# Attention over strided keys: row sums ahead of use, scaling on three engines, and stores of 64 rows of 16 KiB between single loads

## The chip, the cores and the metric

The kernel runs on one core of a Trainium2 chip. The metric is the device time of one execution in microseconds (us). Executions of a program on one core carry the state "fast" when they lie within 1.5% of the fastest of the same kernel, and "slow" above; comparisons below use fast ones.

## The reference

Q, K and V are float32 arrays of 8 x 12 x 1024 x 64. Only every 64th row of K and V takes part, so each of the 96 heads has 16 keys and 16 values, and all 1024 queries of a head attend to the same 16.

```python
def reference(Q, K, V, stride):              # stride = 64
    batch, heads, seq, dim = Q.shape
    scale = 1.0 / np.sqrt(dim)
    for i in range(seq):
        attend_positions = np.arange(0, seq, stride)
        ...
        scores = np.einsum('bhqd,bhkd->bhqk', q, k) * scale
        weights = np.exp(scores - np.max(scores, axis=-1, keepdims=True))
        weights = weights / (np.sum(weights, axis=-1, keepdims=True) + 1e-10)
        result[:, :, i, :] = np.einsum('bhqk,bhkd->bhqd', weights, v)[:, :, 0, :]
```

So 25 MB of Q must be read and 25 MB of output written, with little arithmetic on each byte.

## The kernel before

It works in 24 groups of four heads. A group is one load of 1 MiB of Q, a cast on POOL, a transpose on VectorE, scores on PE, exponentials on ScalarE, sums and outputs on PE, the division on VectorE, and one store of 1 MiB. All transfers are issued by one queue, in order. These parts matter here:

```python
    QBUFS = 10        # groups of Q that can be loaded or on their way
    OBUFS = 9         # buffers of results
    ...
    def sums(g):                                   # 8 matmuls of 4 columns
        sm = psum_s.tile([P, 2, 8, 2], FP32, name="sm", tag="sm")
        for i in range(8):
            nc.tensor.matmul(sm[:, :, i], lhsT=wt[g][:, i], rhs=s_sel, ...)
        nc.vector.reciprocal(rec[g], sm.rearrange("p b i e -> p b (i e)"))

    def outputs(g, c):                             # c = 0 to 3, 512 columns each
        ...
        nc.vector.tensor_tensor(out=out_sb[g][:, :, 4 * c : 4 * c + 4],
                                in0=ps..., in1=rec[g]..., op=ALU.mult)

    def store(g):                                  # 128 rows (partitions) of 8 KiB
        o = out_sb[g]
        _copy(nc, _ap_with(out, [[16 * D, P], [2 * SD, 2], [1, 16 * D]], g * HG * SD),
                  _ap_with(o, [o.ap[0], [1, 1], [1, 32 * D]]))
    ...
    for g in range(NG):
        ...
        store(g)
        if g + QBUFS < NG:
            load(g + QBUFS)
```

"Row" of a store means one partition of the on-chip memory; a store of 128 rows touches all 128 partitions.

The softmax here doesn't subtract the row's maximum and nothing guards it: scores larger than these inputs give would overflow.

## Time and profile before

| | before |
|---|---|
| median of 3 runs | 129.8 us (129.72 to 129.88) |
| span of the profiled run | 127.7 us |
| VectorE / POOL busy | 109.2 us (85%) / 66.7 us (52%) |
| moved over the span | 51.23 MB, 401 GB/s |

The issuing queue's timeline (start, length, issuer, transfer) shows how early stores were queued; loads lie between these lines.

```profile
23.59 0.63 SPq L35 DMA_DIRECT2D out_dram<-out_sb  x1
...
27.57 0.59 SPq L35 DMA_DIRECT2D out_dram<-out_sb  x1
...
31.56 0.59 SPq L35 DMA_DIRECT2D out_dram<-out_sb  x1
```

The ten first loads run until 31.1 us, and the first packet of the first store starts at 30.45 us, so that store was queued 6.2 us ahead of its turn.

### The profile page before, as it was taken

The numbers are of one execution on the slowest core, as the hardware profiler recorded it, in microseconds if no ns is written. First come the engines' busy times: TensorE is split into PE (matmuls) and PEld (weight loads), VectorE is DVE, ScalarE is ACT, GpSimd is POOL, SyncE is SP. The second block draws the span as 40 slices with busy tenths as digits, with TensorE's granted clock in tenths as the row PEclk, the third lists the DMA queues.
The fourth block names the chain that finished last, engine by engine and source line by source line (L and its number), as shares of the span: only waits on it lengthen the run. The fifth ranks groups of instructions, "written<-read, shape, count | busy, mean of one in ns | idle before, by whom it ended". The sixth has DMA issues, their size and how long they took to land. (4 is left out here: it accounts for less than half of the span.)

```text
span 127.7 us, 1518 instructions
## 1 busy us (share of the span) xinstructions
PE 73.3 (57%) x508; PEld 38.6 (30%) x508; DVE 109.2 (85%) x170; ACT 39.6 (31%) x55; POOL 66.7 (52%) x69
## 2 busy tenths in 40 slices
PE   0006767974476097866675579755567776674000
PEld 0003233441433063333342234432234323342000
DVE  6997468999979987899999999999999999999500
ACT  3003404224244134344424440444431344323000
POOL 8980499675217605387767635787555727000000
PEclk9999999999779855599999965799998559999555
DMA  2999989898998998989989999999999999999981
GB/s 70 380 322 459 482 339 482 349 482 359 462 472 336 503 400 377 505 346 431 493 344 439 454 385 436 441 408 452 426 398 464 385 421 431 426 416 428 421 372 46
DMA packets 7913, 51.23 MB, mean 401 GB/s; under 512 B 3872, under 2 KB 3872, under 8 KB 3872
## 3 DMA queue, kind: packets, MB, share of 16 engines
q1 hardware_dynamic: 7904, 51.12, 96.8%
q8 instruction: 4, 0.07, 0.2%
q14 instruction: 5, 0.04, 0.1%
HBM read 25.95 MB, written 25.17 MB: 400 GB/s over the span
## 5 line engine op out<-in xcount | busy, mean ns | idle before, releaser
L254 DVE TENSOR_TENSOR out_sb<-o_ps,rec 128x512 f32<-128x512 f32 x96 | 59.9, 685 | 4.8 <-PE o_ps L249 2.6
L229 ACT ACTIVATE w<-sc 64x512 bf16<-64x512 f32 x48 | 35.1, 732 | 60.0 <-PE sc L218 56.7
L207 POOL CAST qb<-qn 128x2048 bf16<-128x2048 f32 x24 | 45.5, 1898 | 0.4 <-DMA qn<-in_Q_dram 0.4
L249 PE MATMUL o_ps<-vb,w 128*128 128x256 bf16 x192 | 38.0, 321 | 2.4 <-DVE out_sb L254 1.4
L199 POOL TENSOR_TENSOR vb<-mask,v_rep 128x256 bf16<-128x256 bf16 x24 | 16.1, 670 | 40.3 <-PE o_ps L249 35.4
L218 PE MATMUL sc<-qt,k_t 128*128 128x512 bf16 x96 | 32.7, 472 | 1.5 <-DVE qt L211 1.2
L211 DVE STREAM_TRANSPOSE qt<-qb 128x1024 int32<-128x1024 int32 x24 | 29.7, 1237 | 1.6 <-POOL qb L207 1.6
L249 PEld LDWEIGHTS <-w 128*128 128x128 bf16 x192 | 19.3, 110 | 16.2 <-issue 8.6
L238 PE MATMUL sm<-s_sel,w 128*128 128x4 bf16 x192 | 8.7, 167 | 22.1 <-ACT w L229 22.1
L238 PEld LDWEIGHTS <-w 128*128 128x128 bf16 x192 | 6.9, 100 | 30.1 <-ACT w L229 29.6
L218 PEld LDWEIGHTS <-k_t 128*128 128x128 bf16 x96 | 10.8, 114 | 12.0 <-issue 6.5
L169 PE MATMUL kp<-perm_k,k_m 128*128 128x128 bf16 x24 | 3.1, 311 | 17.5 <-DVE k_m L161 17.5
L242 DVE RECIPROCAL rec<-sm 128x32 f32<-128x32 f32 x24 | 7.8, 326 | 0.3 <-PE sm L238 0.3
L169 PEld LDWEIGHTS <-k_m 128*128 128x128 bf16 x24 | 2.3, 141 | 18.2 <-DVE k_m L161 18.2
L177 ACT CAST k_t<-kp 128x512 bf16<-128x512 f32 x6 | 3.2, 590 | 14.1 <-PE kp L169 14.1
L161 DVE TENSOR_SCALAR k_m<-k_raw,slot_m 128x256 bf16<-128x256 f32 x12 | 6.8, 626 | 0.0
L192 DVE CAST v_rep<-vp 128x384 bf16<-128x384 f32 x4 | 2.2, 558 | 2.6 <-PE vp L188 2.6
L135 POOL MEMSET k_t<- 128x4608 bf16 x1 | 3.9, 3938 | 0.0
L145 DVE TENSOR_SCALAR s_sel<-col,slot_f 128x4 bf16<-128x4 int16 x1 | 3.2, 3155 | 0.1
L188 PE MATMUL vp<-v_bf,perm_v 128*128 128x384 bf16 x4 | 2.0, 489 | 0.8 <-DVE v_rep L192 0.6
L177 ACT ACT_TABLE_LOAD x1 | 1.3, 1283 | 2.1 <-DVE k_t L129 2.1
L129 DVE MEMSET k_t<- 128x1152 uint32 x1 | 1.0, 1018 | 1.0 <-PEq L314 1.0
(17 smaller groups left out, 6.3 us busy)
## 6 DMA issues: line engine op xcount, KB each, us to landing
qn<-in_Q_dram SPq DMA_DIRECT2D x24, 1024.0 KB, 13.9
out_dram<-out_sb SPq DMA_DIRECT2D x24, 1024.0 KB, 12.0
k_raw<-in_K_dram SPq DMA_DIRECT2D x1, 384.0 KB, 4.1
v_raw<-in_V_dram SPq DMA_DIRECT2D x1, 384.0 KB, 7.2
```

Source lines behind the costliest of these rows:

```text
L161: nc.vector.tensor_scalar(out=k_m[:, 4 * m : 4 * m + 4, :, h], in0=kr, scalar1=slot_m[:, h : h + 1], scalar2=None, op0=ALU.mult,)
L169: nc.tensor.matmul(kp[:, i, :, f], lhsT=k_m[:, 4 * m + 2 * u + i, f].rearrange("p h q -> p (h q)"), rhs=perm_k.rearrange("p c a b k -> p c ...
L177: nc.scalar.copy(_ap_with(dst, [dst.ap[0], [KW, 8], [32, 4], [1, NK]], extra_offset=NK), kp.rearrange("p i c f (s k) -> p (i c f) s k", s=4),)
L199: nc.gpsimd.tensor_tensor(out=vb[g], in0=mask, in1=v_rep[:, g // 2, g % 2].unsqueeze(1).to_broadcast([P, 4, D]), op=ALU.mult,)
L207: nc.gpsimd.tensor_copy(out=qb[g], in_=qn[g])
L211: nc.vector.transpose(qt[g].bitcast(I32), qb[g].bitcast(I32))
L218: nc.tensor.matmul(sc, lhsT=k_t[:, g, f, NK * (1 - e) : NK * (1 - e) + P], rhs=_ap_with(q, [q.ap[0], [2 * D, 8], [16 * D, 2], [2, 32]], ex ...
L229: nc.scalar.activation(out=_ap_with(wa, [wa.ap[0], [P, 8], [1, 2], [2, 32]], extra_offset=64 * a), in_=sc[64 * a : 64 * a + 64].rearrange( ...
L238: nc.tensor.matmul(sm[:, :, i], lhsT=wt[g][:, i], rhs=s_sel, start=True, stop=True)
L242: nc.vector.reciprocal(rec[g], sm.rearrange("p b i e -> p b (i e)"))
L249: nc.tensor.matmul(ps[:, :, i], lhsT=wt[g][:, 2 * c + i], rhs=vb[g].rearrange("p s d -> p (s d)"), start=True, stop=True,)
L254: nc.vector.tensor_tensor(out=out_sb[g][:, :, 4 * c : 4 * c + 4], in0=ps.rearrange("p b i (e d) -> p b (i e) d", e=2), in1=rec[g][:, :, 4 ...
```

## The change

The change intends to take work off VectorE and to halve the number of packets in a store. Sums are made one group ahead, by four matmuls of 256 columns and a transpose. Of each group's scaling, VectorE keeps three quarters; the last quarter is copied out by ScalarE and multiplied on POOL. Key and value preparation is cut into small steps. Two groups share one result buffer of 2 MiB, and each pair leaves in two stores of 1 MiB: partitions 0 to 63 first, then 64 to 127, each row 16 KiB long, with one load after each. The core of the diff, with cuts:

```diff
-    OBUFS = 9
+    OBUFS = 4
...
-            nc.tensor.matmul(
-                sm[:, :, i], lhsT=wt[g][:, i], rhs=s_sel, start=True, stop=True
-            )
+                sm[32 * q : 32 * q + 32], lhsT=sel32,
+                rhs=wt[g][:, :, 32 * q : 32 * q + 32],
...
+        nc.vector.transpose(
+            smt.rearrange("p i r -> p (i r)"), sm.rearrange("p i r -> p (i r)")
+        )
...
+        if n < 4:
+            nc.scalar.copy(part(i0 + n, 4 - n), ps[:, n:4])
+            nc.gpsimd.tensor_tensor(
+                out=part(i0 + n, 4 - n), in0=part(i0 + n, 4 - n),
+                in1=fact(i0 + n, 4 - n), op=ALU.mult,
+            )
...
-    def store(g):
-        o = out_sb[g]
-            _ap_with(out, [[16 * D, P], [2 * SD, 2], [1, 16 * D]], g * HG * SD),
-            _ap_with(o, [o.ap[0], [1, 1], [1, 32 * D]]),
+    def store(n, h):
+        o = out_2[n][64 * h : 64 * h + 64]
+            _ap_with(out, [[16 * D, 64], [2 * SD, 4], [1, 16 * D]],
+                2 * n * HG * SD + h * SD),
+            _ap_with(o, [o.ap[0], [1, 1], [1, 64 * D]]),
...
-        store(g)
-        if g + QBUFS < NG:
-            load(g + QBUFS)
+        if g % 2 == 1:
+            for h in range(2):
+                store(g // 2, h)
+                if g - 1 + h + QBUFS < NG:
+                    load(g - 1 + h + QBUFS)
```

More of the change, by code (lines that the diff above doesn't have):

```diff
@@ L82 @@
     psum_sc = ctx.enter_context(tc.tile_pool(name="psc", bufs=2, space=bass.MemoryType.PSUM))
-    psum_o = ctx.enter_context(tc.tile_pool(name="po", bufs=4, space=bass.MemoryType.PSUM))
+    psum_o = ctx.enter_context(tc.tile_pool(name="po", bufs=2, space=bass.MemoryType.PSUM))
     psum_s = ctx.enter_context(tc.tile_pool(name="psm", bufs=2, space=bass.MemoryType.PSUM))
@@ L147 @@
     )
+    sel32 = const.tile([P, 32], BF16, name="sel32")
+    nc.vector.memset(sel32, 0.0)
+    nc.vector.tensor_copy(out=sel32[:, 0:4], in_=s_sel)
     slot_m = const.tile([P, 4], FP32, name="slot_m")
@@ L155, with key_rows @@
     v_rep = const.tile([P, NC, 2, D], BF16, name="v_rep")
-    def keys(m):
+    def key_rows(m):
         kr = k_raw[:, 4 * m : 4 * m + 4].rearrange("p n (q f) -> p n f q", f=2)
@@ L164, in keys @@
             )
-        for u in range(2):
-            kp = psum_o.tile([P, 2, 2, 2, 4 * NK], FP32, name="kp", tag="o")
-            for i in range(2):
-                for f in range(2):
-                    nc.tensor.matmul(
-                        kp[:, i, :, f],
-                        lhsT=k_m[:, 4 * m + 2 * u + i, f].rearrange("p h q -> p (h q)"),
-                        rhs=perm_k.rearrange("p c a b k -> p c (a b k)"),
-                        start=True, stop=True,
-                    )
-            g0 = 8 * m + 4 * u
-            dst = k_t[:, g0 : g0 + 4]
-            nc.scalar.copy(
-                _ap_with(dst, [dst.ap[0], [KW, 8], [32, 4], [1, NK]], extra_offset=NK),
-                kp.rearrange("p i c f (s k) -> p (i c f) s k", s=4),
-            )
@@ L183, in value_rows @@
-    def value_rows():
-        nc.vector.tensor_copy(out=v_bf, in_=v_raw)
-        for n in range(2):
-            for c in range(2):
-                vp = psum_sc.tile([P, NC // 2, D], FP32, name="vp", tag="sc")
-                nc.tensor.matmul(
-                    vp, lhsT=perm_v[:, c].rearrange("p a b e k -> p (a b e k)"),
-                    rhs=v_bf[:, 6 * n : 6 * n + 6], start=True, stop=True,
-                )
-                nc.vector.tensor_copy(out=v_rep[:, 6 * n : 6 * n + 6, c], in_=vp)
@@ L194, with keys @@
-    qb, qt, wt, vb, rec, out_sb = {}, {}, {}, {}, {}, {}
+    def keys(m):
+        kp = psum_o.tile([P, 4, 2, 2, 4 * NK], FP32, name="kp", tag="o")
+        for i in range(4):
+            for f in range(2):
+                nc.tensor.matmul(
+                    kp[:, i, :, f],
+                    lhsT=k_m[:, 4 * m + i, f].rearrange("p h q -> p (h q)"),
+                    rhs=perm_k.rearrange("p c a b k -> p c (a b k)"),
+                    start=True, stop=True,
+                )
+        dst = k_t[:, 8 * m : 8 * m + 8]
+        nc.scalar.copy(
+            _ap_with(dst, [dst.ap[0], [KW, 16], [32, 4], [1, NK]], extra_offset=NK),
+            kp.rearrange("p i c f (s k) -> p (i c f) s k", s=4),
+        )
@@ L197, in values, with value_rows @@
+    def value_rows(n):
+        for c in range(2):
+            vp = psum_s.tile([P, NC // 2, D], FP32, name="vp", tag="sm")
+            nc.tensor.matmul(
+                vp, lhsT=perm_v[:, c].rearrange("p a b e k -> p (a b e k)"),
+                rhs=v_bf[:, 6 * n : 6 * n + 6], start=True, stop=True,
+            )
+            nc.vector.tensor_copy(out=v_rep[:, 6 * n : 6 * n + 6, c], in_=vp)
+    qb, qt, wt, vb, rec, out_sb, out_2, o_ps, sm_ps = {}, {}, {}, {}, {}, {}, {}, {}, {}
     def values(g):
@@ L220, in scores @@
                     rhs=_ap_with(
-                        q, [q.ap[0], [2 * D, 8], [16 * D, 2], [2, 32]],
-                        extra_offset=D * e + f,
+                        q, [q.ap[0], [D, 8], [16 * D, 2], [2, 32]],
+                        extra_offset=8 * D * e + f,
                     ),
@@ L233, in scores, with sums_mm, sums_rec @@
             )
-    def sums(g):
-        sm = psum_s.tile([P, 2, 8, 2], FP32, name="sm", tag="sm")
-        for i in range(8):
+    def sums_mm(g):
+        sm = sm_ps[g] = psum_s.tile([P, 8, 32], FP32, name="sm", tag="sm")
+        for q in range(4):
             nc.tensor.matmul(
-                sm[:, :, i], lhsT=wt[g][:, i], rhs=s_sel, start=True, stop=True
-            )
-        rec[g] = rec_pool.tile([P, 2, 16], FP32, name="rec", tag="rec")
-        nc.vector.reciprocal(rec[g], sm.rearrange("p b i e -> p b (i e)"))
+                sm[32 * q : 32 * q + 32], lhsT=sel32,
+                rhs=wt[g][:, :, 32 * q : 32 * q + 32],
+                start=True, stop=True, tile_position=(0, 32 * q),
+            )
+    def sums_rec(g):
+        sm = sm_ps[g]
+        smt = rec_pool.tile([P, 8, 32], FP32, name="smt", tag="smt")
+        nc.vector.transpose(
+            smt.rearrange("p i r -> p (i r)"), sm.rearrange("p i r -> p (i r)")
+        )
+        rec[g] = rec_pool.tile([P, 8, 4], FP32, name="rec", tag="rec")
+        nc.vector.reciprocal(rec[g], smt[:, :, 0:4])
     def outputs(g, c):
         if c == 0:
-            out_sb[g] = out_pool.tile([P, 2, 16, D], FP32, name="out_sb", tag="out_sb")
-        ps = psum_o.tile([P, 2, 2, 2 * D], FP32, name="o_ps", tag="o")
-        for i in range(2):
+            if g % 2 == 0:
+                out_2[g // 2] = out_pool.tile(
+                    [P, 2, 4, 8, D], FP32, name="out_sb", tag="out_sb"
+                )
+            out_sb[g] = out_2[g // 2][:, g % 2]
+        ps = psum_o.tile([P, 4, 4, D], FP32, name="o_ps", tag="o")
+        o_ps[g, c] = ps
+        for i in range(4):
             nc.tensor.matmul(
-                ps[:, :, i], lhsT=wt[g][:, 2 * c + i],
+                ps[:, i].rearrange("p s d -> p (s d)"), lhsT=wt[g][:, 4 * c + i],
                 rhs=vb[g].rearrange("p s d -> p (s d)"),
@@ L253, in outputs, with normalize @@
             )
+    def normalize(g, c):
+        ps = o_ps[g, c]
+        i0 = 4 * c
+        n = 4 if c == 0 else 2
+        part = lambda k, m: out_sb[g][:, :, k : k + m].rearrange("p s i d -> p i s d")
+        fact = lambda k, m: rec[g][:, k : k + m].unsqueeze(3).to_broadcast([P, m, 4, D])
+        if n < 4:
+            nc.scalar.copy(part(i0 + n, 4 - n), ps[:, n:4])
         nc.vector.tensor_tensor(
-            out=out_sb[g][:, :, 4 * c : 4 * c + 4],
-            in0=ps.rearrange("p b i (e d) -> p b (i e) d", e=2),
-            in1=rec[g][:, :, 4 * c : 4 * c + 4].unsqueeze(3).to_broadcast([P, 2, 4, D]),
-            op=ALU.mult,
-        )
-    def store(g):
-        o = out_sb[g]
+            out=part(i0, n), in0=ps[:, 0:n], in1=fact(i0, n), op=ALU.mult
+        )
+        if n < 4:
+            nc.gpsimd.tensor_tensor(
+                out=part(i0 + n, 4 - n), in0=part(i0 + n, 4 - n),
+                in1=fact(i0 + n, 4 - n), op=ALU.mult,
+            )
+    def store(n, h):
+        o = out_2[n][64 * h : 64 * h + 64]
         _copy(
             nc,
-            _ap_with(out, [[16 * D, P], [2 * SD, 2], [1, 16 * D]], g * HG * SD),
-            _ap_with(o, [o.ap[0], [1, 1], [1, 32 * D]]),
-        )
+            _ap_with(
+                out, [[16 * D, 64], [2 * SD, 4], [1, 16 * D]],
+                2 * n * HG * SD + h * SD,
+            ),
+            _ap_with(o, [o.ap[0], [1, 1], [1, 64 * D]]),
+        )
+    key_rows(0)
+    cast(0)
+    cast(1)
+    transpose(0)
     keys(0)
-    cast(0)
-    transpose(0)
+    nc.vector.tensor_copy(out=v_bf, in_=v_raw)
     scores(0)
-    value_rows()
+    transpose(1)
+    value_rows(0)
     values(0)
-    cast(1)
-    transpose(1)
     values(1)
     cast(2)
+    sums_mm(0)
+    sums_rec(0)
     for g in range(NG):
@@ L281 @@
             transpose(g + 2)
-        sums(g)
+        if g + 1 < NG:
+            scores(g + 1)
         outputs(g, 0)
@@ L285 @@
         if g + 1 < NG:
-            scores(g + 1)
-        outputs(g, 2)
-        outputs(g, 3)
+            sums_mm(g + 1)
         if g + 2 < NG:
@@ L292 @@
             cast(g + 3)
-        if g in (2, 4):
-            keys(g // 2)
-        store(g)
-        if g + QBUFS < NG:
-            load(g + QBUFS)
+        normalize(g, 0)
+        normalize(g, 1)
+        if g + 1 < NG:
+            sums_rec(g + 1)
+        if g in (1, 5):
+            key_rows(g // 4 + 1)
+        if g in (2, 6):
+            keys(g // 4 + 1)
+        if g == 3:
+            value_rows(1)
+        if g % 2 == 1:
[3 more added lines that the diff above has]
+                    load(g - 1 + h + QBUFS)
 _INS = ['Q', 'K', 'V', 'stride']
```

## The prediction

> **What bounds the kernel now.** I read the busy tenths first, then the DMA rows, then the waits of the queue that issues transfers, then the groups by line.
>
> ```profile
> DVE  6997468999979987899999999999999999999500
> DMA  2999989898998998989989999999999999999981
> q1 hardware_dynamic: 7904, 51.12, 96.8%
> ```
>
> Two rows are full at once, VectorE and DMA, so busy shares alone don't choose. But VectorE stops with slices 37 and 38, while DMA goes on to the end.
>
> ```profile
> 120.00:127.70 7.70, 0.00 (x0) 0.00 (x0) 0.00 (x0) 0.00 (x0) 0.00 (x0) 0.50 0.59 248
> ```
>
> In this stretch (length, busy time of PE, PEld, DVE, ACT and POOL, clock, DMA share, GB/s) no engine works for the last 7.7 us: queued stores drain. How deep is the queue before that?
>
> ```profile
> SPq L35 <- DVE out_sb L254: 74.5, 22, 9.4
> ...
> qn<-in_Q_dram SPq DMA_DIRECT2D x24, 1024.0 KB, 13.9
> out_dram<-out_sb SPq DMA_DIRECT2D x24, 1024.0 KB, 12.0
> ```
>
> The first line tempts: the issuing queue waits 74.5 us for VectorE. But a 1 MiB store lands 12.0 us after its issue, and in the trace's records of landings one 1 MiB transfer follows another every 2.45 us (36.0 us to 113.8 us holds 32 of them). So about five transfers are always queued, and the wait for VectorE is one that the DMA engines never feel. Per group DMA needs 2 x 2.45 = 4.9 us; VectorE, by the stores' issue times of 66.69 and 70.66 us, needs 3.97 us. The packet records agree: first packet at 1.85 us, last end at 126.26 us, and the packets' times add up to 124.2 us per engine in these 124.4 us. **The bound is DMA, from start to end**; VectorE is second with about 0.9 us a group to spare.
>
> [...] 427 GB/s from 36 to 98 us with loads and stores mixed, 421 GB/s from 101 to 124 us with stores alone.
> [...] The trace has the mask multiply with two inputs, 256 elements in 670 ns[...].
>
> **The change part by part.** Durations are those of the groups by line; those of new shapes are estimates from them.
>
> ```profile
> L254 DVE TENSOR_TENSOR out_sb<-o_ps,rec 128x512 f32<-128x512 f32 x96 | 59.9, 685 | 4.8 <-PE o_ps L249 2.6
> L207 POOL CAST qb<-qn 128x2048 bf16<-128x2048 f32 x24 | 45.5, 1898 | 0.4 <-DMA qn<-in_Q_dram 0.4
> L199 POOL TENSOR_TENSOR vb<-mask,v_rep 128x256 bf16<-128x256 bf16 x24 | 16.1, 670 | 40.3 <-PE o_ps L249 35.4
> L211 DVE STREAM_TRANSPOSE qt<-qb 128x1024 int32<-128x1024 int32 x24 | 29.7, 1237 | 1.6 <-POOL qb L207 1.6
> L242 DVE RECIPROCAL rec<-sm 128x32 f32<-128x32 f32 x24 | 7.8, 326 | 0.3 <-PE sm L238 0.3
> ```
>
> VectorE, a group. Before: transpose 1.24 + reciprocal 0.32 + four scalings in 2.48 (in the timeline bursts of four take 2.48 us) = 4.04 us. After: transpose 1.24; one scaling of 1024 elements, about 2 x 0.62 less one start-up of 0.09 = 1.15; one of 512, 0.65; a transpose of the sums, 256 elements, at a quarter of 1.07 plus 0.17 = 0.44; reciprocal 0.32: together **3.8 us**. A quarter of the scaling leaves, the new transpose takes back half of that.
>
> ScalarE: two exponentials 1.49 us together, plus a copy of 512 elements, about 0.6 (its key copy of that size takes 590 ns): 2.1 us.
>
> POOL: cast 1.90 + mask multiply 0.67 + the new multiply of 512 float32 elements. At the multiply's 2.6 ns an element that is 1.3 us, so **3.9 us**, from 2.57. It becomes as full as VectorE.
>
> PE: 192 loads of the weights for sums go, 4 matmuls of 256 columns replace 8 of 4 columns; at the quick clock I read 109 ns for 256 columns between starts, so about 0.44 us a group for sums, beside 0.87 for outputs and 0.87 for scores. 2.2 us a group, some 4.3 at half clock. Not a bound by itself.
>
> All of this stays under the 4.9 us that DMA needs, so **the compute half of the change is worth about nothing**: it lies beside a full DMA queue.
>
> Start: the first store was issued at 23.6 us with the ten first loads still running until 31.1. Now two groups must be done first. I walked the new order with the durations above (each engine in order, 0.06 us for a semaphore) and get 26 to 28 us for the first pair, then about 37, 47 and 56 us. The queue runs dry at 31.1 and, with four transfers more each time, at 40.9, 50.7 and 60.5. So no hole, with 3 us to spare at least. Small key and value steps help here: before, key steps put 7.2 us between stores (31.56 to 38.80).
>
> End: VectorE then issues its last pair near 115 us; the queue still holds work to about 123, and the last pair of 2.45 us each is inside it. DMA stays the bound.
>
> DMA, packets. The records show stores in 8 KiB packets of 311 ns [...], and loads in 32 KiB packets of 1219 ns. [...] 24 x 0.04 = **1.0 us saved**, if 64 rows move as freely as 128. That gives 129.8 - 1.0 = 128.8 us.
>
> **Rivals.**
> (a) [...] The engines run in step (16 completions of a transfer lie 0.64 us apart early, 1.95 later), so all would be in the same store together[...]. Cost 24 x 2.45 = 59 us: some 187 us. If pairs of engines fall out of step, one loads while the other stores, and the loss shrinks; nothing in the trace says whether they do, since steps of one engine are kept (the spread of 1.95 us lasts from 47 to 104 us). [...] Against it: [...] the order chosen, half-stores with single loads between, looks made to keep reads and writes mixed. I give it two chances in five. Were the loss only partial, 140 to 175 us.
> (b) *POOL or the chain over four engines becomes the bound.* A store now waits for PE, the ScalarE copy, and the POOL multiply, which stands behind a mask multiply and a cast of a later group. If a group takes 4.2 us instead of 3.8, the last pair comes about 22 x 0.4 = 9 us later, at 124, and its two stores need 6 us more: 131 to 134 us. PE at half clock (the clock was 0.5 in 5 of 10 stretches of the trace) would push that way. One chance in ten.
> (c) *The gain is more than packets.* The completions of one transfer spread to 2.4 us by the end; less spread would save perhaps 1 us more, 127.7. Under 127.2 I see little way[...].
>
> **Range and chances.** With rival (a) off and (b) off, 128 to 129.5 us; half of the weight. With (b), 131 to 134. With (a), 140 to 190, around 185. The middle of the whole is near 129.3 us; a range that holds eight in ten has to reach from 127.6 into rival (a)'s full cost, 186. Faster by over 2% (under 127.2): 0.08. Within 2%: 0.50. Slower: 0.42.
>
> **What would show it.** DMA rows: packets fall from 7,913 by 1,536; if the first part holds, the store stretch near the end still moves about 425 GB/s and a 16 KiB packet takes near 612 ns. Near 1,200 ns, with DMA "busy" all through and GB/s well under 400, shows rival (a), and load packets then stay at 1,219 ns. VectorE busy near 103 us rather than 109, POOL near 98 rather than 67. If the queue's waits end on POOL and DMA slices fall below 9 late in the span, rival (b) is right. The prediction goes wrong [...] if the half-stores are spread otherwise over engines than I think, or if POOL's new multiply takes 2 us instead of 1.3.

Passages that rested on statements about the hardware which no trace or run of this case shows are cut from this text, and the cuts are marked. Three sums lose terms by it:

- **Stores.** The forecast came to 129.8 - 24 x 0.04 = 128.8 us. The 0.04 us is a store of eight 8 KiB packets an engine, 8 x 311 ns = 2.49 us, less one of four 16 KiB packets, 2.45 us by the author's 612 ns. From the trace's own packets, 311 ns for 8 KiB and 1,219 ns for 32 KiB, a straight line gives an estimated 614 ns for 16 KiB, and 24 x 0.03 = 0.8 us.
- **Rival (a)** supposes that a store of one half of the partitions runs at half rate, 4.9 us instead of 2.45. No row of the trace before shows it; its cost of 24 x 2.45 = 59 us on 128.8, "some 187 us", stands as an "if".
- **Rival (c).** The least time that seemed possible came to 126 us.

Some small terms stand there without their rows. In the trace before, outputs of 256 columns start 108 to 109 ns apart where the granted clock is 1.0 and 213 ns apart in the median where it is 0.5. Starts of the scalings in a burst lie about 600 ns apart and one takes 685, so 0.09 us is its estimated start-up. An engine starts 0.03 to 0.10 us after the one that released it, in the medians by pair of engines (one pair with a single wait left out).

## More of the kernel before

The rate row of the page cuts the span into 40 slices of 3.2 us and gives GB/s for each; the POOL row gives that engine's busy tenths.

```profile
POOL 8980499675217605387767635787555727000000
GB/s 70 380 322 459 482 339 482 349 482 359 462 472 336 503 400 377 505 346 431 493 344 439 454 385 436 441 408 452 426 398 464 385 421 431 426 416 428 421 372 46
```

The single slices jump between 336 and 505, but they average out.

A view by stretches shows that better. Its columns are: the stretch, its length, busy time of PE, PEld, DVE (VectorE), ACT (ScalarE) and POOL with instruction counts, the granted clock (a share of PE's full speed), the DMA share (how much of the stretch the 16 DMA engines were busy), and GB/s.

```profile
30.00:78.00 48.00, 30.38 (x230) 17.22 (x230) 44.12 (x71) 17.61 (x26) 27.18 (x22) 0.82 1.00 423
78.00:100.00 22.00, 14.67 (x109) 7.53 (x106) 21.46 (x34) 8.55 (x12) 13.28 (x12) 0.89 1.00 425
102.00:122.00 20.00, 10.63 (x84) 5.66 (x82) 17.52 (x29) 5.84 (x8) 3.27 (x4) 0.84 1.01 424
```

The rate is one and the same, 423 to 425 GB/s, in the mixed stretches and in the one with stores alone.

## The result, and the profile after

| | before, same rounds | after |
|---|---|---|
| median | 129.84 us (129.72 to 130.06, 4 runs) | 137.03 us (135.82 to 139.8, 4 runs) |
| ratio of fast runs, 95% interval | | 1.052 (1.0443 to 1.0598): slower |
| span of the profiled run | 127.7 us, clock 0.858 | 135.2 us, clock 0.865 |

A ratio is the mean time of one kernel's fast runs over the mean of the other's in the same rounds, so it isn't quite the ratio of the medians. The run of 139.8 us was a slow one and is not in it; the median of the three fast runs is 136.65 us, so the change costs 6.8 us. The changed kernel's result is correct.

These are the busy tenths and the rates of the page after; a slice is now 3.4 us.

```profile
DVE  6995759999689999689999999999688669860000
POOL 8964499985096995079999999757856958330000
DMA  2999999989799989999999999999999999999940
GB/s 69 364 349 487 397 426 436 436 373 393 291 451 313 334 346 412 431 349 388 363 422 393 390 426 412 451 412 426 412 446 407 426 407 436 409 436 412 412 179 19
```

The DMA row is nearly as full as before. The rate row is not: five slices between 30 and 61 us show 291 to 349 GB/s while the DMA row stands at 7 to 9. The DMA engines are occupied and move less. The same in four stretches (columns as above):

```profile
30.00:78.00 48.00, 33.56 (x192) 17.09 (x193) 44.07 (x63) 23.97 (x34) 35.60 (x31) 0.86 1.00 374
78.00:106.00 28.00, 20.18 (x116) 9.34 (x113) 24.81 (x35) 14.60 (x22) 21.43 (x19) 0.94 1.00 426
106.00:126.00 20.00, 8.53 (x42) 4.06 (x41) 11.76 (x16) 5.28 (x8) 9.08 (x9) 0.74 1.00 422
126.00:135.20 9.20, 0.00 (x0) 0.00 (x0) 0.00 (x0) 0.00 (x0) 0.00 (x0) 0.50 0.42 178
```

The loss can be read off. From 30 to 78 us the DMA share is 1.00 in both kernels, and 374 GB/s stand against 423: 48 us x (423 - 374) / 425 = 5.5 us of transfer not done. From 78 to 126 us nothing is lost. In the drain, 9.20 us at 178 GB/s move what 425 GB/s would move in 3.9 us, so 5.3 us are lost there; the kernel before, 7.70 us at 248, loses 3.2. That is 5.5 + 2.1 = 7.6 us, and the spans differ by 7.5. (Both profiled runs are fast ones.) So the time went in two places, both in DMA: **slow packets early, and an uneven end**.

The packet records of the traces say the same in another way. Per engine, load packets took 57.9 us instead of 54.2, store packets 61.0 instead of 60.0, and idle time was 3.7 us instead of 0.7. Of 2,122 packets of 8 KiB and more that start after 20 us, 120 took over 1.3 times their usual time, three quarters of them from 32 to 65 us; before it was 15 of 3,657. The longest load packet took 3.0 us where 1.23 is usual. A 16 KiB store packet took 616 ns in the median.

One more number from these records will matter. Each transfer has 16 completions, as many as the page counts DMA engines; I take them as one for each engine. I call the distance from the first to the last of them the **spread** of a transfer. Before the first half-store it is 0.84 us; for the load behind that half-store it is 2.44 us, at 51 us it is 4.0, at 71 us 6.1, and at 80 us 7.2, and from there it shrinks slowly to 6.1 us. One transfer takes 2.45 us, so some engines end up nearly three whole transfers behind others. (Completions must be sorted by their transfer, that is, by their semaphore: cut into sixteens in order of time, they can never show more than about one transfer.) In the kernel before, the spread is 0.6 us, then 1.9 from 47 to 101 us, then up to 2.75. The end shows it too: in the changed kernel the engines run out of work one by one, from 127.7 to 133.9 us.

The groups by line (busy time and mean ns of one after the first bar) that answer to those shown of before:

```profile
L280 DVE TENSOR_TENSOR out_sb<-o_ps,rec 128x1024 f32<-128x1024 f32 (+1 forms) x48 | 43.2, 934 | 3.3 <-PE o_ps L266 2.6
L284 POOL TENSOR_TENSOR out_sb<-out_sb,rec 128x512 f32<-128x512 f32 x24 | 25.1, 1044 | 13.5 <-ACT out_sb L279 13.5
...
L279 ACT COPY out_sb<-o_ps 128x512 f32<-128x512 f32 x24 | 14.1, 586 | 5.6 <-DMA out_dram<-out_sb 2.9
...
L165 DVE TENSOR_SCALAR k_m<-k_raw,slot_m 128x256 bf16<-128x256 f32 x12 | 10.8, 956 | 0.0
L249 DVE STREAM_TRANSPOSE smt<-sm 128x256 f32<-128x256 f32 x24 | 10.3, 428 | 0.4 <-PE sm L240 0.4
```

VectorE's scaling fell from 59.9 to 43.2 us and POOL took 25.1 us of new work. All engines are less than 80% busy, and none of them bounds the kernel. One row is worse without having been touched: the key multiply takes 956 ns instead of 626.

The issuing queue's timeline, the stores of the first pair and the first of the second:

```profile
25.70 0.64 SPq L35 DMA_DIRECT2D out_dram<-out_sb  x1
...
27.03 0.59 SPq L35 DMA_DIRECT2D out_dram<-out_sb  x1
...
38.59 0.59 SPq L35 DMA_DIRECT2D out_dram<-out_sb  x1
```

Stores now come in pairs, 13 us apart at the start. The first packet of the second pair's store starts 1.88 us after its issue ends; I call that distance the **lead** of a transfer. The queue is short there, but not dry.

### The profile page after: what moved, and what is told of

The parts are those of the page before. It is cut to its first block, busy times and chain, and to the rows that moved or that the text cites. A ratio compares the mean times of both kernels' runs of the same rounds, so it can differ in the third digit from the quotient of the medians.

```text
span 135.2 us, 1401 instructions
## 1 busy us (share of the span) xinstructions
PE 75.9 (56%) x412; PEld 36.4 (27%) x412; DVE 105.2 (78%) x148; ACT 53.8 (40%) x76; POOL 90.8 (67%) x93
## 2 busy tenths in 40 slices
DMA packets 6375, 51.20 MB, mean 379 GB/s; under 512 B 3872, under 2 KB 3872, under 8 KB 3872
## 4 chain that ended last, share of the span: by engine, by line
DMA 35%; DVE 29%; PE 12%; issue 4%; POOL 3%; SPq 3%; ACT 1%; DVEq 1%; ACTq 0%
DMA out_dram<-out_sb 28%; DVE out_sb L280 13%; DMA qn<-in_Q_dram 7%; DVE k_m L165 6%; DVE qt L213 5%; PE sc L220 5%; PE o_ps L266 5%; POOL qb L209 3%; DVE smt L249 2%; DVE rec L253 2%; SPq L35 2%; PE kp L174 1%; ACT out_sb L279 1%; DVE v_rep L194 1%; PE sm L240 1%
## 5 line engine op out<-in xcount | busy, mean ns | idle before, releaser
L280 DVE TENSOR_TENSOR out_sb<-o_ps,rec 128x1024 f32<-128x1024 f32 (+1 forms) x48 | 43.2, 934 | 3.3 <-PE o_ps L266 2.6
L213 DVE STREAM_TRANSPOSE qt<-qb 128x1024 int32<-128x1024 int32 x24 | 29.0, 1209 | 8.0 <-POOL qb L209 8.0
L284 POOL TENSOR_TENSOR out_sb<-out_sb,rec 128x512 f32<-128x512 f32 x24 | 25.1, 1044 | 13.5 <-ACT out_sb L279 13.5
L266 PE MATMUL o_ps<-vb,w 128*128 128x256 bf16 x192 | 32.0, 307 | 1.1 <-DVE out_sb L280 0.4
L266 PEld LDWEIGHTS <-w 128*128 128x128 bf16 x192 | 19.6, 109 | 18.3 <-DVE out_sb L280 9.5
L279 ACT COPY out_sb<-o_ps 128x512 f32<-128x512 f32 x24 | 14.1, 586 | 5.6 <-DMA out_dram<-out_sb 2.9
L240 PE MATMUL sm<-w,sel 128*32 128x256 bf16 x96 | 13.0, 304 | 4.8 <-ACT w L231 4.1
L165 DVE TENSOR_SCALAR k_m<-k_raw,slot_m 128x256 bf16<-128x256 f32 x12 | 10.8, 956 | 0.0
L249 DVE STREAM_TRANSPOSE smt<-sm 128x256 f32<-128x256 f32 x24 | 10.3, 428 | 0.4 <-PE sm L240 0.4
L253 DVE RECIPROCAL rec<-smt 128x32 f32<-128x32 f32 x24 | 8.5, 353 | 2.3
L240 PEld LDWEIGHTS <-sel 128*32 128x32 bf16 x96 | 4.5, 95 | 15.0 <-issue 13.7
```

The lines of the kernel that those rows point to most:

```text
L165: nc.vector.tensor_scalar(out=k_m[:, 4 * m : 4 * m + 4, :, h], in0=kr, scalar1=slot_m[:, h : h + 1], scalar2=None, op0=ALU.mult,)
L213: nc.vector.transpose(qt[g].bitcast(I32), qb[g].bitcast(I32))
L240: nc.tensor.matmul(sm[32 * q : 32 * q + 32], lhsT=sel32, rhs=wt[g][:, :, 32 * q : 32 * q + 32], start=True, stop=True, tile_position=(0, 3 ...
L249: nc.vector.transpose(smt.rearrange("p i r -> p (i r)"), sm.rearrange("p i r -> p (i r)"))
L266: nc.tensor.matmul(ps[:, i].rearrange("p s d -> p (s d)"), lhsT=wt[g][:, 4 * c + i], rhs=vb[g].rearrange("p s d -> p (s d)"), start=True, ...
L279: nc.scalar.copy(part(i0 + n, 4 - n), ps[:, n:4])
```

## The experiments

Theory A: **half-stores**. Engines that are together in stores of one half of the partitions slow each other, and the loss stays small since engines that collide fall out of step. ("Collide" means no more here than slow packets of several engines at one time.) Rival B: **late issue**. Stores issued in pairs come later, the queue runs short, and that costs; the rows don't matter. Rival C: **compute or packet size**: the chain over four engines, or packets of 16 KiB. "Slow packets" below are those over 1.3 times their usual time (311, 616 and 1,231 ns for 8, 16 and 32 KiB), counted after 20 us.

| run | edit in short | median us (range) | ratio of fast runs | slow packets |
|---|---|---|---|---|
| e1_rows128 | after, 128 rows per store | 132.12 (131.56 to 132.62) | 1.0173 (1.0129 to 1.0217) | 62 |
| e2_evenodd | after, even and odd rows | 136.04 (134.69 to 136.71) | 1.0463 (1.0401 to 1.0525) | 146 |
| e3_onehalf | after, both stores from one half | 160.98 (one run) | none | 728 |
| e4_oldstores | after, stores as before | 129.69 (129.41 to 130.02) | 0.998 (0.9955 to 1.0005) | 11 |
| e5_beforehalves | before, stores in halves | 132.74 (132.13 to 133.92) | 1.0252 (1.0195 to 1.0309) | 73 |
| e7_rows128_8k | e1_rows128 in 8 KiB packets | 132.07 (131.98 to 132.46) | 1.0176 (1.0157 to 1.0194) | 80 |
| e8_offset | after, eight engines set apart | 140.21 (138.72 to 142.29) | 1.0758 (1.0696 to 1.082) | 208 |
| e9_late | e4_oldstores, odd group first | 132.50 (132.17 to 132.73) | 1.019 (1.0165 to 1.0215) | 75 |
| e1_q12 | e1_rows128, 12 query buffers | 129.91 (129.63 to 130.08) | 0.9985 (0.9963 to 1.0007) | 14 |
| after_q12 | after, 12 query buffers | 143.74 (142.31 to 144.24) | 1.1038 (1.0972 to 1.1103) | 314 |
| e1_q11 | e1_rows128, 11 query buffers | 129.34 (129.25 to 130.83) | 0.9994 (0.996 to 1.0028) | 14 |
| after_q11 | after, 11 query buffers | 138.41 (137.33 to 139.5) | 1.0649 (1.0608 to 1.069) | 149 |

Each ratio is against the kernel before in the same rounds. The medians of the changed kernel, e8_offset and after_q11 hold one slow run each; without it they are 136.65, 140.0 and 137.96 us, and the text below works with these. By the rule of 2% e1_rows128, e5_beforehalves and e9_late count as unclear and e7_rows128_8k as the same; but their intervals lie wholly above 1, so the losses are small but clear of noise.

### e1_rows128: the pair in one store of all rows

```diff
-        o = out_2[n][64 * h : 64 * h + 64]
-            _ap_with(out, [[16 * D, 64], ...], 2 * n * HG * SD + h * SD)
+        o = out_2[n]
+            _ap_with(out, [[16 * D, P], ...], 2 * n * HG * SD)
-    store, load, store, load
+    store (2 MiB), load, load
```

> The changed kernel, but each pair of groups goes out in one store of 128 rows of 16 KiB (2 MiB), then two loads. Theory P (partitions): the loss comes from stores that read only one half of the partitions, where engines get in each other's way. Then slow packets (over 700 ns) all but vanish, 16 KiB packets stay near 614 ns, and the time is 128 to 130 us. Rival T (timing): the loss comes from issuing stores only every second group and from the longer chain of engines, so the DMA queue has holes. Then it stays at 136 to 138 us. Rival K (size): 16 KiB packets themselves disturb the 32 KiB loads. Then it also stays at 136 to 138 us with slow load packets.

Measured: 132.12 us. Whole rows give back 4.5 of the 6.8 us (136.65 - 132.12), so the rows matter, which B alone denies. But 2.3 us stay, and they have another form: over half of the slow packets lie in two loads (one of them at 48 to 51.5 us). By the mean of their 16 completions these landed 3.1 and 3.5 us after the one ahead of them, where 2.45 is usual, and each is the second load after a store that was issued with a lead of only 1.1 us. The store packets just before them are in part slow as well, 800 to 1,220 ns at 44 to 46 and at 65 us. The stretch of the first slow load:

```profile
48.00:51.00 3.00, 0.00 (x0) 0.01 (x1) 3.00 (x4) 0.00 (x0) 2.78 (x3) 0.84 1.03 341
```

The DMA share is full and the rate is 341, so this is no empty queue either.

### e2_evenodd: 64 rows spread over the memory

```diff
-        o = out_2[n][64 * h : 64 * h + 64]
+        o = out_2[n]; row = o.ap[0][0]
-            _ap_with(o, [o.ap[0], [1, 1], [1, 64 * D]])
+            _ap_with(o, [[2 * row, 64], [1, 1], [1, 64 * D]], h * row)      (rows of out likewise)
```

> The changed kernel, but the two stores of a pair take the even and the odd partitions instead of the lower and the upper half. Still 64 rows of 16 KiB, same count, same order, same issue times. Theory P, [...] 128 to 130 us and no slow packets [...]. Rivals T and K: nothing they depend on has changed, so 136 to 138 us.

Measured: 136.04 us, a **miss**. I had assumed that even and odd rows cure the loss. Instead the first two stores ran like half-stores: the first two packets of each engine took 616 to 640 ns, the next two mostly 1,000 to 1,270 ns.

```profile
30.00:40.00 10.00, 5.86 (x33) 3.31 (x34) 8.53 (x14) 3.09 (x5) 4.43 (x5) 0.73 0.99 329
```

So spreading 64 rows over the memory didn't help (329 GB/s from 30 to 40 us). Either it counts which rows the engines hold at one time, and I don't know how rows are dealt to engines, or any store of 64 rows is slow, wherever they lie; neither is shown. For the early loss these two aren't told apart; e3_onehalf shows below that the half matters where stores follow each other.

### e3_onehalf: both stores from partitions 0 to 63

Its output is wrong, which doesn't matter for the time. Relative error 1.0: the second store writes the first half's rows again.

```diff
-        o = out_2[n][64 * h : 64 * h + 64]
+        o = out_2[n][0:64]
```

> Wrong result on purpose: both stores of a pair read the lower 64 partitions. Same shapes, count, order. Theory P: engines can no longer escape each other by being one store apart. In the last ten stores, where no load lies between, 16 KiB packets take near 1200 ns and GB/s falls to about 220, so some 155 to 165 us. Rivals T and K: the data's partitions don't matter, 136 to 138 us.

Measured: 160.98 us, one run, so its state is unknown; but it is 24 us off. In the last stretch only stores are left:

```profile
30.00:78.00 48.00, 33.32 (x192) 17.16 (x193) 44.32 (x63) 24.11 (x34) 35.81 (x32) 0.86 1.00 372
78.00:98.00 20.00, 14.04 (x82) 6.53 (x82) 18.12 (x26) 10.60 (x16) 15.90 (x14) 1.00 1.00 389
112.00:155.00 43.00, 6.86 (x32) 3.16 (x30) 8.37 (x12) 3.85 (x6) 6.61 (x6) 0.50 0.98 208
```

208 GB/s (said: about 220) is half of 426, with packets of 16 KiB at about 1,200 to 1,290 ns, twice 616. This is the loss of theory A by itself: **stores that all read one half of the partitions ran at half rate, 208 GB/s against 422 with alternating halves**. Size, order and the places written in `out` are those of the changed kernel, so the number of rows and the pattern of the writes, which a half-store changes too, can't explain this difference. Spread alone doesn't help either: here it was 7.3 to 7.6 us, and each store still landed 5.0 us after the one ahead.

Up to 78 us, where single loads lie between these one-half stores, the rate was 372 GB/s, as in the changed kernel (374), and from 78 to 98 us it was 389, where the changed kernel had 426. So, I conclude, loads between them shelter the stores, but only in part; the rest of the shelter is the other half, since engines that are stores apart can be reading opposite halves. In the changed kernel's stretch of stores alone (106 to 126 us, 422 GB/s) it is the only one.

### e4_oldstores: the new compute with stores as before

```diff
-        o = out_2[n][64 * h : 64 * h + 64]
-            _ap_with(out, [[16 * D, 64], [2 * SD, 4], ...], 2 * n * HG * SD + h * SD)
+        o = out_2[n][:, h]
+            _ap_with(out, [[16 * D, P], [2 * SD, 2], ...], (2 * n + h) * HG * SD)
```

> The changed kernel with the stores of before: 128 rows of 8 KiB for one group, but issued at the same points (two after every second group, one load after each). Theory P: 129 to 130.5 us, as before, since the compute part hides beside DMA. Rival T: still 136 to 138 us, since issue times and compute are those of the changed kernel. Rival K: 129 to 130.5 us.

Measured: 129.69 us, the same as before. Everything new on PE, VectorE, ScalarE and POOL is in this kernel, so rival C's chain over four engines costs nothing, and the relief of VectorE earns nothing.

```profile
30.00:78.00 48.00, 33.15 (x194) 17.02 (x194) 44.34 (x62) 24.29 (x35) 35.98 (x31) 0.87 1.01 423
```

My expectation had a flaw, though. I wrote that stores are issued at the same points; the timeline says otherwise, since the first group's store doesn't wait for the second group:

```profile
22.14 0.63 SPq L35 DMA_DIRECT2D out_dram<-out_sb  x1
...
25.61 0.59 SPq L35 DMA_DIRECT2D out_dram<-out_sb  x1
...
32.90 0.59 SPq L35 DMA_DIRECT2D out_dram<-out_sb  x1
```

So this run changed rows and issue together, and doesn't separate A from B. Three runs below do.

### e5_beforehalves: the old kernel with halves

```diff
+        for h in range(2):
+            o = out_sb[g][64 * h : 64 * h + 64]
-            _ap_with(out, [[16 * D, P], ...], g * HG * SD)
+            _ap_with(out, [[16 * D, 64], ...], g * HG * SD + h * SD)
```

> The kernel before with nothing changed but the store: each group's 128 rows of 8 KiB go out as two stores of 64 rows of 8 KiB, lower and upper half of the partitions, then the load. Theory P [...]: slow packets appear with the old compute and the old packet size too, and the time rises by 2 to 8 us, to 132 to 138 us. If instead the change's compute or the 16 KiB packets were needed for the loss, it stays at 129.8 us[...].

Measured: 132.74 us. Old compute, old packets of 8 KiB, stores issued at the end of every group as before, and only the rows are halved: 2.5% slower (interval 1.0195 to 1.0309), with 73 slow packets, over half of them at 30 to 50 us.

```profile
30.00:50.00 20.00, 11.54 (x92) 7.06 (x93) 17.54 (x31) 6.54 (x10) 8.47 (x7) 0.83 0.97 380
50.00:100.00 50.00, 34.30 (x262) 18.43 (x261) 48.82 (x76) 19.01 (x26) 31.80 (x27) 0.86 1.01 427
```

That is the picture of the changed kernel in small: a lossy stretch, then 418 to 427 GB/s until the stores drain. The spread jumps from 0.6 us at the last load before the stores to 3.8 at the first load behind them and stays at 3.7 to 4.4 until 125 us. Halves alone do harm, which speaks for A and against B and C as the only cause.

### e7_rows128_8k: the packet size

```diff
-            _ap_with(o, [o.ap[0], [1, 1], [1, 64 * D]])
+            _ap_with(o, [o.ap[0], [32 * D, 2], [1, 32 * D]])     (on e1_rows128)
```

> As the run with one 2 MiB store of 128 rows per pair of groups (132.1 us), but each row is read in two pieces of 8 KiB instead of one of 16 KiB. It asks where that run's remaining 3.3 us of slow packets come from. If from the packet size: none here, 129 to 130.3 us. If from the order (2 MiB of store, then two loads): 131 to 133 us again.

Measured: 132.07 us against 132.12. With whole rows, packets of 8 or 16 KiB made no difference; what remains of rival C falls.

### e8_offset: engines set apart beforehand

If engines that fall out of step stop colliding, setting eight of them one transfer behind before the first half-store ought to spare the collisions.

```diff
+        if g == QBUFS - 1:            # the tenth load in three transfers
+            for a in range(3):
+                p, n = (32 * a, 8) if a < 2 else (64, 16)
+                _copy(nc, qn[g][p : p + 4 * n], ...)
+            return
```

> The changed kernel, with its half-stores of 64 rows as they are; only the tenth load is dealt otherwise: its lower 64 partitions come in two transfers of 8 rows, [...] its upper 64 in one of 16 rows. That puts 8 engines one 1 MiB transfer (2.45 us) behind the other 8 before the first store. Theory P [...] slow packets all but vanish, and the time is 129 to 132 us (the 8 engines carry 32 KiB more than the average, 1.2 us). If [...] the loss has another cause, it stays at 135 to 138 us.

Measured: 140.21 us, a **miss**.

```profile
29.00:33.00 4.00, 0.76 (x8) 0.86 (x9) 4.00 (x6) 0.00 (x0) 2.63 (x3) 0.72 1.00 356
```

The eight engines ahead were alone in the half-store, the other eight still loading at their usual 1,231 ns a packet; and yet the four packets of each of the eight took 616, 616, 616 to 1,253, and 1,399 to 1,553 ns. So, if engines in the same store are what slows each other, those that do so lie within these eight. Which engines slow which was my assumption, and no run shows it. The packet records carry no engine number, so the pairs can't be read from them.

### e9_late: late issue with whole rows

```diff
-        o = out_2[n][:, h]
+        o = out_2[n][:, 1 - h]                     (on e4_oldstores; rows of out likewise)
```

> The run with the old store shape (129.7 us) turned out to send the even group's store one group earlier than the changed kernel does, so it changed two things. This one keeps 128 rows of 8 KiB for one group, but sends the odd group's store first, so that, as in the changed kernel, nothing is issued before both groups of the pair are done. Theory P alone: still 129.5 to 130.3 us, no slow packets. Theory P with timing (a store that is issued when the queue is almost dry makes a later load slow, as both slow loads of the 128-row run followed a store issued 1.1 us before its data): 131 to 133 us. Timing alone: 136 us or more.

The odd group's store goes first, so nothing can be issued before a pair is done. Rows, size and compute are those of e4_oldstores. Measured: 132.50 us against 129.69. Two places are slow (landings by the mean of 16 completions). The load after a store with a lead of 1.43 us landed 2.96 us after that store; later a store with a lead of 1.12 us landed 3.07 us after its forerunner, and the load behind it 3.37 us after that. That store has all 128 rows, and yet many of its packets took 600 to 642 ns, twice 311: doubled packets aren't a mark of half-stores alone. So B is real: **late issue costs about 2.8 us by itself**, close in size and form to what was left in e1_rows128.

### e1_q12, after_q12, e1_q11, after_q11: more query buffers

An eleventh or twelfth load in flight lengthens the queue and so the lead. Twelve buffers fit only with three result buffers instead of four; eleven fit with four if the raw values borrow one.

```diff
-    QBUFS = 10
-    OBUFS = 4
+    QBUFS = 12                        (e1_q12, after_q12)
+    OBUFS = 3
...
-    QBUFS = 10
-    v_raw = const.tile([P, NC, D], FP32, name="v_raw")
+    QBUFS = 11                        (e1_q11, after_q11)
+    v_raw = out_pool.tile([P, 2, 4, 8, D], FP32, name="v_raw", tag="out_sb")
```

> One 2 MiB store of 128 rows of 16 KiB per pair, with 12 query buffers and 3 output buffers of a pair. If both causes are named rightly (partition halves, late issue), this removes both and keeps the larger packets: 128.5 to 129.5 us, the best so far. If the 2 MiB store costs by itself: 131 to 132.5 us.

> The changed kernel with its half-stores, but 12 query buffers instead of 10 (and 3 output buffers of a pair instead of 4, to make room): two more loads, 4.9 us of work, are queued before the first store, so no store is issued to a nearly dry queue. Timing alone: 129 to 130 us. Theory P alone: 135.5 to 137.5 us, no better. Both: 133 to 135.5 us.

> One 2 MiB store of 128 rows of 16 KiB per pair, with 11 query buffers and all 4 output buffers of a pair (the raw values borrow an output buffer's room). The second store then has some 3.6 us in hand instead of 1.1, and the end isn't short of output buffers as in the run with 12 and 3 (whose last three stores found the queue dry, with about 1.7 us lost). If late issue and half-stores are the two causes: few slow packets and 128.5 to 129.6 us, a little below both kernels. If 3.6 us are too little: 130.5 to 132.

> The changed kernel with its half-stores, with 11 query buffers and all 4 output buffers, so the queue neither runs low early nor late; it is the pair of the run above. In the run with 12 and 3 buffers the queue ran dry at 107 us, all engines stood in step again, and the last half-stores collided anew (143.7 us); that can't happen here. Half-stores alone (theory P): 133 to 136 us, with slow packets early and few after 80 us. If late issue was all of the loss: 129 to 130 us.

Measured with whole rows: 129.91 us with 12 and 129.34 with 11 (median of six runs, one of them 130.83), against 132.12 with 10. With eleven, the leads of the second and fourth store are 3.44 and 2.69 us instead of 1.14 and 1.08, and the two slow loads are gone:

```profile
30.00:78.00 48.00, 32.57 (x194) 16.74 (x194) 44.34 (x63) 24.17 (x35) 35.85 (x31) 0.87 1.00 422
102.00:122.00 20.00, 8.04 (x51) 3.81 (x48) 12.27 (x19) 6.45 (x10) 6.65 (x6) 0.80 1.01 427
```

With halves the same buffers gain nothing: 137.96 us with 11 (fast runs), 143.74 with 12. The stretch of after_q11 (its profiled run fell in the slow state, so only the rate next to 422 is read here, not the time):

```profile
30.00:78.00 48.00, 32.51 (x192) 16.68 (x193) 44.34 (x63) 24.06 (x34) 35.83 (x32) 0.87 1.00 384
```

The loss is there with a long queue too. In after_q12 three result buffers were too few: its queue ran dry near 107 us, and at 109 us half of the engines stood idle. So the engines came back into step (the spread fell from 7.8 to 1.2 us), and the half-stores collided anew to the end.

```profile
107.50:135.00 27.50, 15.14 (x86) 7.29 (x84) 19.79 (x29) 10.88 (x16) 14.44 (x14) 0.81 0.97 293
```

Only stores are left in it, as in the changed kernel's stretch of 422 GB/s, where the engines were still apart; and the DMA share of 0.97 shows that the queue wasn't empty for most of it. The same half-stores ran at 293 GB/s after a restart in step, and at 422 without one.

The four corners, medians of fast runs in us:

| | 10 query buffers | 11 query buffers |
|---|---|---|
| halves of 64 rows | 136.65 | 137.96 |
| all 128 rows | 132.12 | 129.34 |

Whole rows gain 4.5 us with the short queue and 8.6 with the long one. The long queue gains 2.8 us with whole rows and nothing with halves. So the halves are the cause of the loss, enough by themselves; late issue is a second cost, which shows once the halves are gone. The best version, e1_q11, is not faster than the kernel before (ratio 0.9994), and no run was.

## Why the prediction was right or wrong

The interval held 137.03 us, but the point, 129.3, missed by 7.7 us, and "within 2%" at 0.50 was the wrong side of a near even split with "slower" at 0.42. That the interval held is partly luck: none of the prediction's cases names 137 us (128 to 129.5, 131 to 134, 140 to 190). It lies in the gap between them, and the interval reached over that gap only because it had to take in rival (a) at full cost.

**The bound.** Right. From 30 to 126 us the DMA share is 1.00, and the engines stand idle in the last 9.2 us.

**Compute worth about nothing.** Right, shown by e4_oldstores: the whole new compute with the old stores gives a ratio of 0.998. Single costs: transpose of the sums 428 ns (said 0.44 us, as 0.17 fixed and a quarter of 1.07; the 1,024-element transpose took 1,209 ns here, so an estimated 0.17 fixed and 0.26 for 256 elements), scalings 1,191 ns for 1,024 elements and 676 for 512 (1.15 and 0.65 us), copy 586 ns (0.6), first pair issued at 25.70 us (26 to 28), packets 7,913 to 6,375 (1,538 fewer, said 1,536). VectorE came to 105.2 us busy where 103 was said; the key multiply's 12 x 0.33 us = 4.0 us more is the part that wasn't in the sum. POOL came to 90.8 us (said 98), since its new multiply took 1,044 ns, not 1.3 us: 2.0 ns an element, where the mask multiply of other types and size takes 2.6 (670 ns for 256). Two slips change nothing: the new transpose takes back two thirds of VectorE's relief by the prediction's own terms (0.44 of 0.68 us), not half, and the spread at the end of the kernel before is 2.5 to 2.75 us, not 2.4.

**"No hole, with 3 us to spare at least."** Half wrong. No hole came, but the second pair was issued at 38.59 us instead of 37 and the fourth at 59.50 instead of 56; the lead was 1.88 us. Before the second pair stand four key multiplies, 4.07 us in all (the page of the kernel before has 626 ns for one, so 2.5 us), which is the size of what the walk missed; why they got slower isn't shown. I also held that any lead above zero is enough. e9_late and e1_rows128 show transfers that take 3.0 to 3.5 us at and after stores issued with 1.1 to 1.4 us of lead, worth 2 to 3 us in all.

**"1.0 us saved, if 64 rows move as freely as 128."** The packet's length was right (616 ns in the median, said 612, or 614 by the trace's own packets); the condition failed. With whole rows and a long queue (e1_q11) store packets took 59.3 us per engine against 60.0, so 0.6 us.

**Rival (a), the step that failed.** Its half rate is real, and e3_onehalf shows it by itself: 208 GB/s and about twice 616 ns; by what mechanism isn't shown. Its size was wrong: the term "24 x 2.45 = 59 us" stood on engines that stay in step, with "steps of one engine are kept" read from the kernel before. There hardly anything collided (15 slow packets of 3,657), so hardly anything could push engines apart. In the changed kernel they were 2.44 us apart one transfer after the first half-store and 7.2 us apart at 80 us, and the cost was 6.8 us (7.5 between the profiled runs: 5.5 us of slow transfer until 78 us, and 2.1 us at the end, where engines that are transfers apart finish apart, from 127.7 to 133.9 us). The branch "if pairs fall out of step, the loss shrinks" was in the text, but with 140 to 175 us, whose middle of 157.5 us is 27.7 over the time before, still about four times too dear. What would have shown it: an alternation of load and half-store has an order, colliding engines a transfer or more apart, in which they no longer read the same half at once, and the collisions themselves push engines towards it. That they push them there is argued from the spread and the rates, in the changed kernel, in e5_beforehalves and after the restart of after_q12; that the stream then runs without loss is measured (426 and 422 GB/s).

**Rivals (b) and (c).** No sign of either. In the list of what the issuing queue waited for (total us, number, longest), POOL has a small row:

```profile
SPq L35 <- DVE out_sb L280: 47.6, 9, 12.9
...
SPq L35 <- POOL out_sb L284: 4.1, 4, 2.9
```

**Open.** How the rows of a 64-row store are dealt to the engines (e2_evenodd and e8_offset both missed, perhaps over it), and whether even and odd rows lose early for the same reason as halves; why a store issued about 1.1 us before its turn makes a later load slow, of which the coincidence and the cure by one more buffer are shown and no mechanism; and why the first two packets of a half-store still take 616 ns.

## What to carry to other kernels

When DMA bounds a kernel, keep every store on all 128 partitions: stores of half of them were slow here wherever the engines that read one half at a time stood together (374 GB/s against 423 early on, 208 from one half alone), and a DMA row full of nines hides that, so read GB/s by stretches beside it. Put the same stretch with only one part of the change into a run of its own before crediting or blaming the rest, and check in the timeline that the part really came alone. A steady spread in an undisturbed trace said nothing here about how a disturbance grows or settles: 1.9 us from 47 to 101 us in the kernel before, up to 7.2 us in the changed one.
